# Empty transposes first, token transposes among memory products, rotary tables on GpSimd, and a norm factor kept at -2 times its value

## Chip, core and metric

One core of a Trainium2 chip. The metric is the device time of one launch in microseconds, as the median of several executions. TensorE (PE) does matmuls and transposes, VectorE (DVE), ScalarE (ACT) and GpSimd (POOL) work element by element, and SyncE (SP) issues most of the DMAs.

## What is computed

A decoder trunk of two layers over 1024 tokens of width 1024. Both layers also attend to 256 memory tokens; layer 0 uses latent attention with rotary positions, layer 1 a sliding window. Only the parts that the change touches are quoted.

```python
def rmsnorm(x, g):
    xf = x.astype(jnp.float32)
    y = xf * lax.rsqrt(jnp.mean(xf * xf, axis=-1, keepdims=True) + EPS)
    return (y * g.astype(jnp.float32)).astype(x.dtype)

def rope(x, positions):
    ...
    inv = ROPE_THETA ** (-(jnp.arange(half, dtype=jnp.float32) * 2.0) / r)
    ang = positions.astype(jnp.float32)[..., None] * inv
    cos = jnp.cos(ang)[:, :, None, :]
    sin = jnp.sin(ang)[:, :, None, :]
    ...

def memory_cross_attention(q_cross, mem_n, w_mem_kv):
    b, s, _ = q_cross.shape
    kv = (mem_n @ w_mem_kv).reshape(b, N_MEM, 2, MEM_HEADS, HEAD_DIM)
    ...

    mem_n = rmsnorm(mem, mem_norm_g)
    for i in range(DEPTH):
        j = i // 2
        hn = rmsnorm(x, attn_norm_g[i])
        ...
        cross = memory_cross_attention(q_cross, mem_n, w_mem_kv[i])
        x = x + jnp.concatenate([mix, cross], axis=-1) @ w_o[i]
        x = x + squared_relu_mlp(rmsnorm(x, mlp_norm_g[i]), mlp_w_up[i], mlp_w_down[i])
    return rmsnorm(x, final_norm_g)
```

## The kernel before

Every operand that must be exact is kept as a high and a low half (`split`: ScalarE writes the rounded high half, VectorE the difference), and a product is three matmuls. Tokens stand in eight tiles of 128, weights in slices of 128 rows.

The start. `ident`, the identity for transposes, is built on GpSimd. `mem_T` loads the two memory tiles, transposes a block of 45 rows with all gains (`gains`, from five small DMAs on ScalarE's queue), and for each tile computes the norm factor (`rstd_of`: square with a running sum on ScalarE, mean plus EPS on VectorE, then `newton`), scales it, transposes it in two groups of four and multiplies by the gain on the way out of PSUM. `mem_kv(0)` makes the keys and values of the memory for layer 0: four groups of 16 matmuls in float32, 128x256. Then the first two token tiles are loaded, the input weights `mla_w_in` come slice by slice through two raw buffers and are split, `mem_kv(1)` makes layer 1's memory keys and values, `rope_tables` reduces the angles on VectorE in some 60 small steps and takes two sines on ScalarE, and `masks` builds two masks.

The loop over tokens comes behind that: `a_norm` (factor and scaling), `a_T` (eight transposes, split into `xhls`), `a_in` (the input product, 8 slices of six matmuls into a buffer `ps2` of which there are two; then the norm factors of the compressed parts and the rotation of the key with the tables), `a_cT` (transposes of the result). Buffers `ps1` are four PSUM slots that all small products and transposes share.

Norm factors are a root and a reciprocal with one Newton step, r(1.5 - 0.5 r r z). `Rstd` does the same for the output and MLP phases and for the final norm: `half` squares each half of a row, `get` forms the factor: two sums and EPS on VectorE, root on ScalarE, four small steps on VectorE.

The order on each engine is found at build time by a list scheduler that has its own model of durations; at run time each engine and each DMA queue works strictly in that order. `issue_after` adds an order on one engine, `high_priority` raises a group.

In the kernel's last stage (`Down.run`, layer 1) the final gain is loaded into `gt`; after the last matmul of a token tile come the sum with the residual, the square of the second half, `get`, and a scaling by factor and gain, which is stored.

Of the kernel before, what the change touches and what calls it, by code (L numbers as in the profile page):

```python
# [19 lines left out]
P = 128  # L20
# [35 lines left out]
def trunk(  # L56
# [38 lines left out]

    def split(src, hi, lo, scale=None):

        if scale is None:
            nc.scalar.activation(hi, src, AF.Copy)  # L99
            nc.vector.tensor_tensor(lo, src, f32(hi), ALU.subtract)  # L100
        else:
            nc.scalar.activation(hi, src, AF.Copy, scale=scale)
            nc.vector.scalar_tensor_tensor(lo, src, scale, f32(hi), ALU.mult, ALU.subtract)
# [23 lines left out]

    def masks(pl):

        nc.vector.tensor_copy(identb, ident)  # L130
        for dst, sgn in ((dmask, 1), (dmaskT, -1)):
# [3 lines left out]
            nc.vector.tensor_copy(dst, m)  # L135
# [16 lines left out]
    def gains(pl):  # L152
        grow = pl.tile([45, P], F32, name="grow")
        for src, r in ((mem_norm_g, 37), (attn_norm_g, 0), (mlp_norm_g, 16), (mla_q_norm_g, 32), (mla_kv_norm_g, 35)):
            n = 8 if r == 37 else src.shape[0] * src.shape[1] // P
            nc.scalar.dma_start(out=grow[r : r + n, :], in_=src.rearrange("(k p) -> k p" if len(src.shape) == 1 else "l (k p) -> (l k) p", p=P))
        pt = ps1("psg")[:, 0:45]
        nc.tensor.transpose(pt, grow, ident[0:45, 0:45])
        nc.vector.tensor_copy(gcol, pt)

    small_ct = [0]

    def rstd_of(pl, src_parts, junk):
# [22 lines left out]
    def rstd_halves(pl, xt, junk):  # L186

        small_ct[0] += 1
        ss = pl.tile([P, 2], F32, tag="ss", bufs=4, name=f"ss{small_ct[0]}")
        for i, c in enumerate((slice(0, 512), slice(512, 1024))):  # L190
            nc.scalar.activation(junk[:, c], xt[:, c], AF.Square, accum_out=ss[:, i : i + 1])
        z = pl.tile([P, 2], F32, tag="zs", bufs=4, name=f"zs{small_ct[0]}")[:, 0:1]
        nc.vector.tensor_scalar(z, ss[:, 0:1], ss[:, 1:2], 1.0 / D, ALU.add, ALU.mult)
        nc.vector.tensor_scalar(z, z, EPS, None, ALU.add)
        return newton(pl, ss, z, 1)
# [26 lines left out]
    def rope_tables():  # L222
        tp = pool("ropet")
        V = nc.vector
# [12 lines left out]

        def less(acc, k, c):
            V.scalar_tensor_tensor(acc, k, -c, acc, ALU.mult, ALU.add)

# [9 lines left out]
        def reduced_prod(h, c):  # L250
# [4 lines left out]
            for pc, qc in zip(parts(c, 12, 4), parts(TWO_PI, 12, 4)):  # L255
                V.scalar_tensor_tensor(acc, h, pc, acc, ALU.mult, ALU.add)
# [4 lines left out]
        with tc.issue_after(mem_end[0].ins):  # L261
            V.tensor_copy(posf, pos_i)
# [17 lines left out]
        nc.scalar.activation(sinb.rearrange("p t j -> p (t j)"), th, AF.Sin)  # L280
# [1875 lines left out]
```

## Time and profile before

| | us |
|---|---|
| median of 3 runs | 2117.09 (2114.58 to 2121.81) |
| the profiled execution | 2116.59 |
| its span in the profile | 2114.9 |
| TensorE busy / VectorE / ScalarE / GpSimd | 2078.4 / 1470.6 / 1134.6 / 159.6 |

The page gives for each engine the time in which it worked. TensorE's share says how little can be won, its waits say where, and the windows with the granted clock say where it worked at half speed (0.50 is 1.2 GHz, 1.00 is 2.4 GHz). Matmuls overlap in the records, so the distance between starts, not the duration of one, is their pace.

### The profile page before, as it was taken

Reading aid. Unit: us, or ns where it says so; the run is one execution under the profiler, and the core shown is the slowest. Engines: PE = TensorE matmul, PEld = TensorE weight load, DVE = VectorE, ACT = ScalarE, POOL = GpSimd, SP = SyncE. Lnnn points to the kernel's source line nnn. Section 1 sums busy time; section 2 is a strip of 40 time slices with the busy share of each in tenths; the row PEclk is TensorE's granted clock in tenths of the full one; section 3 lists DMA queues with packets and bytes.
Section 4 is the critical chain, followed back from the end, with each engine's and each line's share of the span. In section 5 each row is a group of like instructions: output and inputs, shape, how many; then the busy total and the mean of one; then the engine's idle time right before and its main releaser. Section 6 shows DMA issues by size and latency. Waiting matters only on the chain.

```text
span 2114.9 us, 29110 instructions
## 1 busy us (share of the span) xinstructions
PE 2078.4 (98%) x9928; PEld 1708.0 (81%) x9928; DVE 1470.6 (70%) x2833; ACT 1134.6 (54%) x2444; POOL 159.6 (8%) x224
## 2 busy tenths in 40 slices
PE   7999999999999999999999999999999999999998
PEld 6988777788788878888888878778888878788886
DVE  7555588865977776976657553866976775976565
ACT  5455477776754443444445553976745443444452
POOL 0013100001000000000001241620000000000000
PEclk9999999999999999999999999999999999999999
DMA  7202123342354446944433241242344446844342
GB/s 247 68 1 76 46 65 92 105 143 100 110 170 162 140 136 218 337 159 143 150 119 95 66 146 54 81 137 73 133 146 159 157 139 230 317 151 155 118 122 85
DMA packets 177070, 282.92 MB, mean 134 GB/s; under 512 B 17581, under 2 KB 73370, under 8 KB 176922
## 3 DMA queue, kind: packets, MB, share of 16 engines
q1 hardware_dynamic: 170480, 265.30, 39.2%
q0 software_dynamic: 4016, 13.12, 1.8%
q10 hardware_dynamic: 2426, 2.65, 0.4%
q8 instruction: 78, 1.28, 0.3%
q14 instruction: 70, 0.57, 0.1%
HBM read 187.47 MB, written 81.05 MB: 127 GB/s over the span
## 4 chain that ended last, share of the span: by engine, by line
PE 80%; DVE 7%; DMA 6%; ACT 4%; issue 2%; SPq 0%; POOL 0%; DVEq 0%; ACTq 0%; POOLq 0%
PE psy L1805 5%; PE psy L1803 5%; PE psy L1804 5%; PE psz L1805 4%; PE psz L1803 4%; PE psz L1804 4%; PE pss L930 4%; PE pso L972 4%; PE psu L1468 3%; PE psu L1470 3%; PE psu L1469 3%; DMA mr<-in_mlp_w_up_dram 3%; PE pswo L108 3%; PE pswo L110 3%; PE pswo L109 2%; PE psf L108 2%
## 5 line engine op out<-in xcount | busy, mean ns | idle before, releaser
L1368 ACT ACTIVATE mr<-mr,gcol 128x256 f32<-128x256 f32 (+1 forms) x160 | 67.3, 477 | 81.2 <-DMA mr<-in_mlp_w_up_dram 77.5
L1368 ACT ACTIVATE d<-d,gcol 128x256 f32<-128x256 f32 x128 | 57.7, 499 | 79.0 <-DMA d<-in_mlp_w_up_dram 61.7
L1803 PE MATMUL psy<-g 128*128 128x512 f32 x256 | 99.9, 390 | 0.0
L1804 PE MATMUL psy<-g 128*128 128x512 f32 x256 | 99.6, 389 | 0.0
L1805 PE MATMUL psy<-g 128*128 128x512 f32 x256 | 99.4, 389 | 0.0
L99 ACT ACTIVATE g<-i 128x512 fp32r<-128x512 f32 x79 | 49.6, 628 | 89.1 <-PE psz L1804 46.3
L100 DVE TENSOR_TENSOR g<-i,g 128x512 fp32r<-128x512 f32 x79 | 55.5, 703 | 48.9 <-ACT g L99 48.9
L99 ACT ACTIVATE uh<-i 128x512 fp32r<-128x512 f32 x66 | 41.6, 630 | 86.1 <-PE psy L1804 40.7
L99 ACT ACTIVATE i<-mr 128x512 fp32r<-128x512 f32 x78 | 49.1, 629 | 70.8 <-PE psy L1804 20.6
L951 ACT ACTIVATE p<-pss 128x512 f32<-128x512 f32 x108 | 63.6, 593 | 41.1 <-PE pss L930 41.0
L100 DVE TENSOR_TENSOR pl<-p,ph 128x512 fp32r<-128x512 f32 (+1 forms) x96 | 61.5, 651 | 27.4 <-ACT ph L99 26.9
L805 DVE TENSOR_REDUCE m<-psx 128x1 f32<-128x128 f32 (+5 forms) x96 | 70.1, 747 | 11.0 <-PE psx L801 10.8
L100 DVE TENSOR_TENSOR uh<-i,uh 128x512 fp32r<-128x512 f32 x66 | 45.6, 690 | 44.7 <-ACT uh L99 44.7
L1804 PE MATMUL psz<-g 128*128 128x512 f32 x192 | 74.7, 389 | 0.0
L1805 PE MATMUL psz<-g 128*128 128x512 f32 x192 | 74.7, 389 | 0.0
L1803 PE MATMUL psz<-g 128*128 128x512 f32 x192 | 74.7, 389 | 0.0
L100 DVE TENSOR_TENSOR i<-mr,i 128x512 fp32r<-128x512 f32 x78 | 53.6, 687 | 22.0 <-ACT i L99 21.6
L1684 DVE TENSOR_TENSOR mqf<-mqq,mqf 128x512 f32<-128x512 f32 x64 | 43.1, 686 | 21.9 <-DMA mqq<-in_mlp_w_down_dram 21.7
L99 ACT ACTIVATE ph<-p 128x512 fp32r<-128x512 f32 (+1 forms) x96 | 56.4, 599 | 1.3
L1805 PEld LDWEIGHTS psy<-g 128*128 128x128 f32 x256 | 48.1, 188 | 10.0
L1804 PEld LDWEIGHTS psy<-g 128*128 128x128 f32 x256 | 48.1, 188 | 9.9
L1803 PEld LDWEIGHTS psy<-g 128*128 128x128 f32 x256 | 48.1, 188 | 9.8
(658 smaller groups left out, 6913.4 us busy)
## 6 DMA issues: line engine op xcount, KB each, us to landing
i<-hd SPq DMA_DIRECT2D x154, 256.0 KB
hd<-uh SPq DMA_DIRECT2D x76, 256.0 KB
hd<-ul SPq DMA_DIRECT2D x76, 256.0 KB
mr<-in_mlp_w_up_dram SPq DMA_DIRECT2D x36, 512.0 KB
hd<-x SPq DMA_DIRECT2D x72, 256.0 KB
mr<-hd SPq DMA_DIRECT2D x70, 256.0 KB
d<-in_mlp_w_up_dram SPq DMA_DIRECT2D x32, 512.0 KB
mqq<-in_mlp_w_down_dram SPq DMA_DIRECT2D x32, 512.0 KB
```

What stands on the lines that cost most here:

```text
L99: nc.scalar.activation(hi, src, AF.Copy)
L100: nc.vector.tensor_tensor(lo, src, f32(hi), ALU.subtract)
L108: nc.tensor.matmul(ps, ah, bh, start=first and i == 0, stop=False)
L110: nc.tensor.matmul(ps, al, bh, start=False, stop=last and i == n - 1)
L805: nc.vector.reduce_max(m8s[h][:, i : i + 1], ps[:, c], axis=AX, negate=True)
L930: return lambda: nc.tensor.matmul(o, a, b, skip_group_check=True, **kw)
L951: nc.scalar.activation(p, ps, AF.Exp, scale=SC)
L972: mms.append(lambda: nc.tensor.matmul(o, a, b, skip_group_check=True, **kw))
L1368: nc.scalar.activation(w[:, k, :], w[:, k, :], AF.Copy, scale=g_mlp[layer][:, k0 + k : k0 + k + 1])
L1803: nc.tensor.matmul(ps, ah[:, j, :], bh, start=p in (1, 5, 2) and k == 0, stop=False, skip_group_check=True)
L1804: nc.tensor.matmul(ps, ah[:, j, :], bl, start=False, stop=False, skip_group_check=True)
L1805: nc.tensor.matmul(ps, al[:, j, :], bh, start=False, stop=k == NP - 1, skip_group_check=True)
```

## The change

Transposes: `idle(n)` transposes the identity n times into a PSUM buffer that nobody reads: 24 ahead of everything, 10 between the two memory tiles, 8 ahead of the memory products. The memory's gains are loaded and transposed on their own first. The first two token tiles are normalised ahead of the weight splits and transposed between the groups of `mem_kv(1)`, whose weight loads are issued behind the fourth input slice; raw buffers for input weights become four; tokens 2 and 3 are loaded right behind the weights. The masks are built at the start and cast behind the memory tiles.

Rotary tables: all steps go to GpSimd, a fused multiply-add becomes two steps, and the two sines are put behind the last memory copy, the last split and the last root on ScalarE.

Norm factors: the root is taken from the sum itself (scale and EPS inside the activation), the Newton step becomes (t - 3) r, which is -2 times the factor, and all gains are scaled by -0.5. `Rstd` adds EPS to the first half's sum on GpSimd, feeds that to the root of the second sum as its bias, and forms z on GpSimd.

```diff
+    ends = [None, None]
+
     def split(src, hi, lo, scale=None):
 
         if scale is None:
-            nc.scalar.activation(hi, src, AF.Copy)
+            ends[1] = nc.scalar.activation(hi, src, AF.Copy)
...
+    built = []
+
     def masks(pl):
 
-        nc.vector.tensor_copy(identb, ident)
         for dst, sgn in ((dmask, 1), (dmaskT, -1)):
             m = pl.tile([P, P], F32, tag="mask", bufs=2, name=f"mask{sgn}")
             nc.gpsimd.memset(m, 0.0)
             nc.gpsimd.affine_select(out=m, in_=m, compare_op=ALU.is_ge, fill=NEG, base=0, pattern=[[-sgn, P]], channel_multiplier=sgn)
-            nc.vector.tensor_copy(dst, m)
+            built.append((dst, m))
+
+    def masks_cast():
+        with tc.issue_after(mem_end[0].ins):
+            nc.vector.tensor_copy(identb, ident)
+            for dst, m in built:
+                nc.vector.tensor_copy(dst, m)
...
+    def gains(pl, srcs, at, name):
+        n = sum(int(np.prod(src.shape)) // P for src in srcs)
+        grow = pl.tile([n, P], F32, name=f"grow{name}")
+        r = 0
+        for src in srcs:
+            k = int(np.prod(src.shape)) // P
+            nc.scalar.dma_start(out=grow[r : r + k, :], in_=src.rearrange("(k p) -> k p" if len(src.shape) == 1 else "l (k p) -> (l k) p", p=P))
+            r += k
+
+        def turn():
+            pt = ps1(f"psg{name}")[:, 0:n]
+            nc.tensor.transpose(pt, grow, ident[0:n, 0:n])
+            nc.vector.tensor_scalar(gcol[:, at : at + n], pt, -0.5, None, ALU.mult)
+
+        return turn
...
+    root = [None]
 
     def rstd_of(pl, src_parts, junk):
 
         k = len(src_parts)
         small_ct[0] += 1
-        ss = pl.tile([P, 2], F32, tag="ss", bufs=4, name=f"ss{small_ct[0]}")
-        z = pl.tile([P, 2], F32, tag="zs", bufs=4, name=f"zs{small_ct[0]}")
+        ss, z, rs, t = [pl.tile([P, 2], F32, tag=n, bufs=4, name=f"{n}{small_ct[0]}") for n in ("ss", "zs", "rs", "rt")]
         for i, (ap, n) in enumerate(src_parts):
-            nc.scalar.activation(junk[:, :n], ap, AF.Square, accum_out=ss[:, i : i + 1])
-            nc.vector.tensor_scalar(z[:, i : i + 1], ss[:, i : i + 1], 1.0 / n, EPS, ALU.mult, ALU.add)
-        return newton(pl, ss, z[:, :k], k)
-
-    def newton(pl, ss, z, k):
-
-        rs = pl.tile([P, 2], F32, tag="rs", bufs=4, name=f"rs{small_ct[0]}")
-        rk, t = rs[:, :k], ss[:, :k]
-        nc.scalar.activation(t, z, AF.Sqrt)
+            c = slice(i, i + 1)
+            nc.scalar.activation(junk[:, :n], ap, AF.Square, accum_out=ss[:, c])
+            root[0] = nc.scalar.activation(t[:, c], ss[:, c], AF.Sqrt, scale=1.0 / n, bias=eps_t)
+            nc.vector.tensor_scalar(z[:, c], ss[:, c], 1.0 / n, EPS, ALU.mult, ALU.add)
+        rk, t, z = rs[:, :k], t[:, :k], z[:, :k]
         nc.vector.reciprocal(rk, t)
-        nc.vector.tensor_tensor(t, rk, rk, ALU.mult)
-        nc.vector.tensor_tensor(t, t, z, ALU.mult)
-        nc.vector.tensor_scalar(t, t, -0.5, 1.5, ALU.mult, ALU.add)
-        nc.vector.tensor_tensor(rk, rk, t, ALU.mult)
+        if k == 1:
+            nc.vector.scalar_tensor_tensor(t, rk, z, rk, ALU.mult, ALU.mult)
+        else:
+            nc.vector.tensor_tensor(t, rk, rk, ALU.mult)
+            nc.vector.tensor_tensor(t, t, z, ALU.mult)
+        nc.vector.scalar_tensor_tensor(rk, t, -3.0, rk, ALU.add, ALU.mult)
         return rs
...
-        V = nc.vector
+        V = nc.gpsimd
...
+        def add(acc, k, c):
+            n[0] += 1
+            r = tp.tile([P, NT * 16], F32, tag="add", bufs=2, name=f"rt{n[0]}")
+            V.tensor_scalar(r, k, c, None, ALU.mult)
+            V.tensor_tensor(acc, acc, r, ALU.add)
+
         def less(acc, k, c):
-            V.scalar_tensor_tensor(acc, k, -c, acc, ALU.mult, ALU.add)
+            add(acc, k, -c)
...
+        with tc.issue_after(ends[0].ins), tc.issue_after(ends[1].ins), tc.issue_after(root[0].ins):
+            nc.scalar.activation(sinb.rearrange("p t j -> p (t j)"), th, AF.Sin)
+            nc.scalar.activation(hs, th, AF.Sin, scale=0.5)
...
+    def mem_kv_steps(layer, kv, memT, pl):
...
+            ends[0] = nc.scalar.activation(kv.v[:, t, :], ps, AF.Copy)
+            yield
...
-        gains(pl)
+        turns = [gains(pl, [mem_norm_g], 37, "m"), gains(pl, [attn_norm_g, mlp_norm_g, mla_q_norm_g, mla_kv_norm_g], 0, "")]
+        turns[0]()
         for t in range(2):
             y = pl.tile([P, D], F32, tag="y", bufs=2, name=f"ym{t}")
-            rs = rstd_of(pl, [(xs[t], D)], y)
+            with tc.issue_after(root[0].ins):
+                rs = rstd_of(pl, [(xs[t], D)], y)
             nc.vector.tensor_scalar(y, xs[t], rs[:, 0:1], None, ALU.mult)
+            if t:
+                idle(10)
             for a in range(0, KT, 4):
                 ps = ps1(f"psTm{t}_{a}")
                 for i in range(4):
                     nc.tensor.transpose(ps[:, i * P : (i + 1) * P], y[:, (a + i) * P : (a + i + 1) * P], ident)
                 mem_end[0] = nc.vector.tensor_tensor(mT[:, a : a + 4, t * P : (t + 1) * P], ps.rearrange("p (k c) -> p k c", k=4), g_mem[:, a : a + 4].unsqueeze(2).to_broadcast([P, 4, P]), ALU.mult)
+        turns[1]()
+        idle(8)
         return mT
...
+    root[0] = nc.scalar.activation(warm, eps_t, AF.Sqrt)
+    def idle(n):
+        pw = ps1(f"psnone{n}")
+        for _ in range(n):
+            nc.tensor.transpose(pw[:, 0:P], ident, ident)
+
+    idle(24)
+    masks(pm)
     memT = mem_T(pm)
     small_loads()
     mem_kv(0, kv0, memT, pm)
...
+    def a_norm(t):
+        norm_y(pa, xts[t], fa0[:, 2 + t % 2, :])
+        if 1 < t < NT - 2:
+            xts.append(load_x(t + 2))
...
     xts = [load_x(0), load_x(1)]
+    a_norm(0)
+    a_norm(1)
     wih = pa.tile([P, KT, MLA_IN], F32R, name="wih")
     wil = pa.tile([P, KT, MLA_IN], F32R, name="wil")
     for kt in range(KT):
-        raw = f1[:, kt % 2, 0:MLA_IN]
+        raw = f1[:, kt % 4, 0:MLA_IN]
         nc.sync.dma_start(out=raw, in_=mla_w_in[0, kt * P : (kt + 1) * P, :])
         split(raw, wih[:, kt, :], wil[:, kt, :], scale=g_attn[0][:, kt : kt + 1])
-    mem_kv(1, kvt, memT, pm)
+        if kt == 3:
+            mem1 = mem_kv_steps(1, kvt, memT, pm)
+            next(mem1)
+    xts += [load_x(2), load_x(3)]
+    for t, _ in enumerate(mem1):
+        if t < 2:
+            a_T(t)
+    a_norm(2)
+    masks_cast()
     rope_tables()
-    masks(pm)
...
-    a_norm(0)
-    for k in range(NT + 2):
-        if k < NT:
+    for k in range(1, NT + 2):
+        if 1 < k < NT:
             a_T(k)
-        if k + 1 < NT:
+        if 1 < k < NT - 1:
             with tc.high_priority(offset=120):
                 a_norm(k + 1)
...
+            self.n = 0
+
+        def half(self, x_, junk):
+            ss = self.st[:, self.n : self.n + 1]
+            nc.scalar.activation(junk, x_, AF.Square, scale=1.0 / 32.0, accum_out=ss)
+            if self.n == 0:
+                nc.gpsimd.tensor_scalar(self.st[:, 5:6], ss, EPS, None, ALU.add)
+            self.n += 1
 
         def get(self):
-            ss, z, rk, t = self.st[:, 0:2], self.st[:, 2:3], self.st[:, 3:4], self.st[:, 4:5]
-            nc.vector.tensor_scalar(z, ss[:, 0:1], ss[:, 1:2], EPS, ALU.add, ALU.add)
-            nc.scalar.activation(t, z, AF.Sqrt)
+            ss, z, rk, t, z0 = [self.st[:, i : i + 1] for i in (1, 2, 3, 4, 5)]
+            nc.scalar.activation(t, ss, AF.Sqrt, bias=z0)
+            nc.gpsimd.tensor_tensor(z, ss, z0, ALU.add)
             nc.vector.reciprocal(rk, t)
             nc.vector.scalar_tensor_tensor(t, rk, z, rk, ALU.mult, ALU.mult)
-            nc.vector.tensor_scalar(t, t, -0.5, 1.5, ALU.mult, ALU.add)
-            nc.vector.tensor_tensor(rk, rk, t, ALU.mult)
+            nc.vector.scalar_tensor_tensor(rk, t, -3.0, rk, ALU.add, ALU.mult)
             return rk
...
             if layer == 1:
                 gt = m.raw()
                 nc.scalar.dma_start(out=gt.rearrange("p a c -> p (a c)"), in_=final_norm_g.partition_broadcast(P))
+                nc.gpsimd.tensor_scalar(gt, gt, -0.5, None, ALU.mult)
```

In `rope_tables` the other fused multiply-add (acc + h pc) is `add(acc, h, pc)` too, and `posf` no longer waits for the memory tiles. The definitions of `xhls`, `a_norm` and `a_T` move up unchanged but for the line shown; `rstd_halves`, which nothing called, goes.

## Rows read from the trace of the kernel before

**Rows 1.** The page, part 1: busy us, share of the span, instructions.
```profile
PE 2078.4 (98%) x9928; PEld 1708.0 (81%) x9928; DVE 1470.6 (70%) x2833; ACT 1134.6 (54%) x2444; POOL 159.6 (8%) x224
```

**Rows 2.** Waits of TensorE over the span: total us, times, longest us.
```profile
PE psg L158 <- DMA grow<-in_mla_kv_norm_g_dram: 9.7, 1, 9.7
PE psT_a L207 <- DVE kml L334: 2.4, 2, 1.6
...
PE psT_m L1286 <- ACT d L1275: 1.2, 2, 1.0
```

**Rows 3.** TensorE in order of time, 0 to 64: start us, us, count.
```profile
9.90 3.55 PE L444 MATMUL psTm<-ident,ym 128*128 128x128 f32 x16
13.50 7.17 PE L319 MATMUL pskm<-memT,wm 128*128 128x256 f32 x32
...
34.33 7.07 PE L326 MATMUL psvm<-wm,memT 128*128 128x256 f32 x32
...
47.64 0.78 PE L117 MATMUL psin<-wih,xhls 128*128 128x512 f32 x1
...
56.68 0.39 PE L117 MATMUL psin<-wih,xhls 128*128 128x512 f32 x1
...
57.94 0.39 PE L117 MATMUL psin<-wih,xhls 128*128 128x512 f32 x1
```

**Rows 4.** The chain that ended last, in order of time: start us, us.
```profile
59.36 0.87 PE psT_a L207 x8
```

**Rows 5.** Windows: us, busy by engine, granted TensorE clock, DMA share, GB/s.
```profile
48.00:50.00 2.00, 2.00 (x6) 1.68 (x6) 0.84 (x3) 1.97 (x4) 0.00 (x0) 0.50 0.83 260
```

**Rows 6.** GpSimd, ScalarE and VectorE in order of time, 0 to 62.
```profile
2.24 0.31 POOL L125 TENSOR_SCALAR_AFFINE_SELECT ident<-ident 128x128 f32<-128x128 f32 x1
...
4.55 1.06 ACT L170 ACTIVATE ym<-mem 128x1024 f32<-128x1024 f32 x1 [1.62 <-DMA mem<-in_mem_dram]
...
7.08 0.52 ACT L178 ACTIVATE ss<-zs 128x1 f32<-128x1 f32 x2
...
8.39 0.86 DVE L440 TENSOR_SCALAR ym<-mem,rs 128x1024 f32<-128x1024 f32 x1
...
12.76 1.42 DVE L445 TENSOR_TENSOR memT<-psTm,gcol 128x512 f32<-128x512 f32 x2 [0.16 <-PE psTm L444]
...
15.10 0.17 DVE L262 CAST posf<-pos_i 128x8 f32<-128x8 int32 x1 [0.93 <-DMA pos_i<-in_positions_dram]
...
30.59 1.18 DVE L103 SCALAR_TENSOR_TENSOR wil<-fa,gcol,wih 128x928 fp32r<-128x928 f32 x1 [1.69 <-ACT wih L102]
```

**Rows 7.** Windows of 20 us, the first: columns as in rows 5.
```profile
0.00:20.00 20.00, 10.29 (x47) 9.21 (x48) 11.23 (x59) 8.09 (x15) 2.60 (x15) 1.00 0.95 286
```

**Rows 8.** GpSimd's groups by shape: count, busy us, mean ns, idle before.
```profile
L303 POOL TENSOR_TENSOR fa<-fa,rb 128x192 f32<-128x192 f32 x8 | 5.7, 711 | 0.0
...
L1976 POOL CAST df<-di 128x128 f32<-128x128 int32 x1 | 0.3, 287 | 0.0
```

**Rows 9.** Instructions on the rotary tables: ns min/median/max, first and last start.
```profile
L239 DVE SCALAR_TENSOR_TENSOR rt<-rt,rt x18: 272/285/293, 17.1 to 40.1; 128x128 f32<-128x128 f32 x18
...
L256 DVE SCALAR_TENSOR_TENSOR rt<-rt,rt x8: 283/285/288, 17.9 to 33.0; 128x128 f32<-128x128 f32 x8
```

**Rows 10.** Instructions that read the cosine table, the first group of rotations.
```profile
L298 DVE TENSOR_TENSOR fa<-psin,cosb x8: 168/174/175, 68.2 to 145.6; 128x16 f32<-128x16 f32 x8
```

**Rows 11.** All engines in order of time, around 1120.
```profile
1120.19 0.48 DVE L1785 TENSOR_SCALAR d<-g,sinb 128x512 f32<-128x512 f32 x1
...
1120.53 1.89 POOL L1902 TENSOR_TENSOR wsr<-wsr,gcol 128x1024 f32<-128x1024 f32 x1 [3.18 <-DMA wsr<-in_swa_w_in_dram]
1120.58 2.12 DVE L1785 TENSOR_SCALAR d<-d,sinb 128x512 f32<-128x512 f32 x1
```

**Rows 12.** VectorE in order of time, the last norm factor.
```profile
2108.58 0.21 DVE L1199 TENSOR_SCALAR cosb<-cosb 128x1 f32<-128x1 f32 x1 [0.79 <-ACT i L1195]
...
2109.52 0.15 DVE L1203 TENSOR_SCALAR cosb<-cosb 128x1 f32<-128x1 f32 x1
```

More of the change, by code (lines that the diff above doesn't have):

```diff
@@ L150, in trunk @@
     g_q, g_kv, g_mem = gcol[:, 32:35], gcol[:, 35:37], gcol[:, 37:45]
[L152 to L159, printed above, removed]
+    def gains(pl, srcs, at, name):
[11 more added lines that the diff above has]
+        return turn
     small_ct = [0]
+    root = [None]
     def rstd_of(pl, src_parts, junk):
@@ L255, in reduced_prod @@
             for pc, qc in zip(parts(c, 12, 4), parts(TWO_PI, 12, 4)):
-                V.scalar_tensor_tensor(acc, h, pc, acc, ALU.mult, ALU.add)
+                add(acc, h, pc)
                 less(acc, k, qc)
@@ L260, in rope_tables @@
         posf = tp.tile([P, NT], F32, name="posf")
-        with tc.issue_after(mem_end[0].ins):
-            V.tensor_copy(posf, pos_i)
+        V.tensor_copy(posf, pos_i)
         ang = tmp()
@@ L309, in mem_kv @@
     def mem_kv(layer, kv, memT, pl):
+        for _ in mem_kv_steps(layer, kv, memT, pl):
+            pass
+    def mem_kv_steps(layer, kv, memT, pl):
         wsrc = w_mem_kv[layer].rearrange("(k p) n -> p k n", p=P)
@@ L322, in mem_kv @@
                 dup_split(ps[e * 64 : e * 64 + 64], kv.kh[:, h, :], kv.kl[:, h, :])
+        yield
         for t in range(2):
@@ L326, in mem_kv @@
                 nc.tensor.matmul(ps, memT[:, kt, t * P : (t + 1) * P], wv[:, kt, :], start=kt == 0, stop=kt == KT - 1)
-            nc.scalar.activation(kv.v[:, t, :], ps, AF.Copy)
+            ends[0] = nc.scalar.activation(kv.v[:, t, :], ps, AF.Copy)
+            yield
     def dup_split(ps, kh, kl):
@@ L473, in trunk @@
     warm = pm.tile([P, 1], F32, name="warm")
-    nc.scalar.activation(warm, eps_t, AF.Sqrt)
+    root[0] = nc.scalar.activation(warm, eps_t, AF.Sqrt)
[5 more added lines that the diff above has]
+    masks(pm)
     memT = mem_T(pm)
@@ L485, in load_x, with a_T @@
         return xt
+    xhls = quad_tile("q0", "xhls", F32R)
+    xT, cs_ = {}, {}
+    def a_norm(t):
+        norm_y(pa, xts[t], fa0[:, 2 + t % 2, :])
+        if 1 < t < NT - 2:
+            xts.append(load_x(t + 2))
+    def a_T(t):
+        y = fa0[:, 2 + t % 2, :]
+        xhl = [xhls[:, 2 * (t % 2) + i, :].rearrange("p (k c) -> p k c", k=KT) for i in range(2)]
+        xh, xl = xhl
+        T_split(y, lambda a: (xh[:, a : a + 4], xl[:, a : a + 4]), f"a{t}")
+        xT[t] = (xh, xl)
     xts = [load_x(0), load_x(1)]
+    a_norm(0)
+    a_norm(1)
     wih = pa.tile([P, KT, MLA_IN], F32R, name="wih")
@@ L537, in trunk @@
     CQC, CKR = 640, 896
-    xhls = quad_tile("q0", "xhls", F32R)
-    xT, cs_ = {}, {}
-    def a_norm(t):
-        norm_y(pa, xts[t], fa0[:, 2 + t % 2, :])
-        if t + 2 < NT:
-            xts.append(load_x(t + 2))
-    def a_T(t):
-        y = fa0[:, 2 + t % 2, :]
-        xhl = [xhls[:, 2 * (t % 2) + i, :].rearrange("p (k c) -> p k c", k=KT) for i in range(2)]
-        xh, xl = xhl
-        T_split(y, lambda a: (xh[:, a : a + 4], xl[:, a : a + 4]), f"a{t}")
-        xT[t] = (xh, xl)
     def a_in(t):
@@ L1192, in __init__ @@
             self.st = st[:, small_ct[0] % 8, :]
-        def half(self, i, x_, junk):
-            nc.scalar.activation(junk, x_, AF.Square, scale=1.0 / 32.0, accum_out=self.st[:, i : i + 1])
+            self.n = 0
[5 more added lines that the diff above has]
+            self.n += 1
         def get(self):
-            ss, z, rk, t = self.st[:, 0:2], self.st[:, 2:3], self.st[:, 3:4], self.st[:, 4:5]
-            nc.vector.tensor_scalar(z, ss[:, 0:1], ss[:, 1:2], EPS, ALU.add, ALU.add)
-            nc.scalar.activation(t, z, AF.Sqrt)
+            ss, z, rk, t, z0 = [self.st[:, i : i + 1] for i in (1, 2, 3, 4, 5)]
+            nc.scalar.activation(t, ss, AF.Sqrt, bias=z0)
+            nc.gpsimd.tensor_tensor(z, ss, z0, ALU.add)
             nc.vector.reciprocal(rk, t)
             nc.vector.scalar_tensor_tensor(t, rk, z, rk, ALU.mult, ALU.mult)
-            nc.vector.tensor_scalar(t, t, -0.5, 1.5, ALU.mult, ALU.add)
-            nc.vector.tensor_tensor(rk, rk, t, ALU.mult)
+            nc.vector.scalar_tensor_tensor(rk, t, -3.0, rk, ALU.add, ALU.mult)
             return rk
@@ L1272, in norm @@
             t = TORD[p]
-            rst[t].half(1, xb, y[:, 1, :])
+            rst[t].half(xb, y[:, 1, :])
             rs = rst.pop(t).get()
@@ L1317, in sum0 @@
                 rst[t] = Rstd()
-                rst[t].half(0, x_, m.t(f"d{3 + p % 2}")[:, 0, :])
+                rst[t].half(x_, m.t(f"d{3 + p % 2}")[:, 0, :])
             xs = {0: load(0, half), 1: load(1, half)}
@@ L1733, in stat @@
                     nc.gpsimd.dma_start(out=x1[ts, i * 512 : i * 512 + 512], in_=xs[i])
-                    r.half(i, xs[i], y[i])
+                    r.half(xs[i], y[i])
                 def fin():
@@ L1780, in norm @@
                 for i in (1, 0):
-                    r.half(i, xs[i], y[i])
+                    r.half(xs[i], y[i])
                 rs = r.get()
```

11 lines of the change are left out of this document (removed).

## The prediction

> **What bounds the kernel now.** I read the page first: TensorE is busy for 98% of the span [rows 1], so only time in which it stands still, or runs at the lower clock, can be won. Next the waits of TensorE over the whole span, longest first [rows 2]: one of 9.7 us before its first instruction, 2.4 us ahead of the first token transposes, and from there on nothing above 1.2 us in one place. The change touches the start, the norm factors all along and the end, so I then read the start in order of time, with the clock. Three things are to be seen there. First, the 16 memory transposes take 3.55 us [rows 3], 0.222 us each, where eight token transposes later take 0.87 us [rows 4], 0.109 each: they run at 1.2 GHz, though the clock column shows no drop so early. The memory products follow without a gap from 13.50 to 41.40 [rows 3]. Second, between 41.40 and the third token's transposes at 59.36 [rows 3, 4] lie 17.96 us, in which TensorE does 16 transposes and one token's input product. At full speed that is 16 x 0.109 = 1.74, and eight steps of 57.94 - 56.68 = 1.26 us, 10.08: together 11.82. So 6.1 us are lost: part as waits for PSUM buffers that a crowded VectorE frees late [rows 2], the rest because the granted clock after them is 0.50 (1.2 GHz), as late as 50 [rows 5]. Third, the memory tokens: ScalarE starts the first square at 4.55, but both roots come at 7.08, behind the second square, and the first normalised tile is written only at 8.39 [rows 6].
>
> **The change, part by part.** The sum is made against the profiled execution, 2116.59 us, span 2114.9, so 1.69 lie around the span; it is 0.5 below the median of the three runs, 2117.09.
>
> *Start of the memory products, 13.50 now.* The square of tile 0 ends at 4.55 + 1.06 = 5.6, some 5.7 with its sum. The root now follows it, with no VectorE step between: 0.25, then three small steps of about 0.2 each [rows 12], then 0.86 for the tile [rows 6]: 7.4 to 7.5 instead of 9.25. Its eight transposes take 0.9 at the full clock. Tile 1's root is where both were, 7.08 plus its time; its factor is there at 8.0 and the tile at 8.8, its transposes done at 9.7. From 7.5 on VectorE has tile 1's small steps (0.6), its scaling (0.86) and four multiplications by the gain, 0.71 each (1.42 for two, [rows 6]); the first product needs three of these four: 11.1, the last is done at 11.8. I take 11.3. Bounds: 10.0 if only tile 1's first multiplication follows its transposes, 12.3 if all 42 empty transposes stand ahead of the 16 real ones (2.55 + 24 x 0.222 + 18 x 0.109 + 1.74 + 0.71). The 24 first ones start when the identity is ready, at 2.55 [rows 6]; at 0.222 they end by 7.9, and sooner once the clock rises. TensorE has nothing else to do then, so I cost them at nothing; without that cover the 42 cost 42 x 0.109 = 4.6. The gain row for the memory now has its own transpose, ahead of tile 0: if that small DMA lands as late as the last of the five did (9.7, [rows 2]), 2 us of this part are gone. Gain 2.2, between 0.2 (that) and 3.5.
>
> *From there to the third token's transposes.* Memory products 27.9, 16 token transposes 1.74, one input product 10.08: 39.7 with no wait, so 11.3 + 39.7 = 51.0 instead of 59.36. The token transposes now stand between products, which hide the emptying of their PSUM buffers: the 6.1 us lost there should not come back. Gain of both parts together 8.4.
>
> *Is the data there?* SyncE's queue now has, ahead of the second layer's memory keys: 1.05 MB memory, 2.1 MB first memory weights, 1.05 MB tokens, 1.9 MB input weights; with the keys 7.15 MB. At the 286 GB/s of the first 20 us [rows 7] they have landed at 25.0; their halves are needed at 25.2 and 26.1. The rest, to the last input weight (10.1 MB), lands at 35.3 and is split by 37.6; the input product needs its first step at 40.9 and its last after 49. So it fits, with about 1 us to spare in the first place.
>
> *Rotary tables on GpSimd.* VectorE is rid of 26 multiply-adds of 0.285 [rows 9] and the other steps on the tables. [...] Up to the sine: 16 small columns and 41 steps with one input, at no more than 0.29, and 28 with two. For these the trace has 0.29 (one input, same size) and 0.71 (two inputs, half as wide again) as ends [rows 8]; I take 0.45, nearer by size. 57 x 0.29 + 28 x 0.45 = 29.1 us from the landing of the positions, 15.10 [rows 6]: 44.2, by the ends 39.7 to 51.5. Sine, its table and two closing steps add 2.6. The first rotation stands at 68.2 now [rows 10], at 59.8 after a shift of 8.4, and the third input product needs its PSUM buffer back at about 62.7. So the tables are hidden, by 6 to 17 us. Behind the sines on ScalarE's queue stand the squares and roots of token 0 and the high halves of token 2: they have the same slack. Roots and sines still alternate once, so table loads are as many as now.
>
> Against this part speaks what happens when GpSimd and VectorE read together: a 128x512 scaling takes 0.48 us at 1120.19 and 2.12 at 1120.58, where a GpSimd product of 1.89 began 0.05 earlier [rows 11]. So whichever starts second may wait for the whole of the other. In the window VectorE has eight low halves of the input weights, 1.18 each, and three scalings of 0.86 [rows 6]: at most 12 us that GpSimd can lose, so the angles come at 56.2 at worst from 44.2, and at 63.5 from 51.5; only the last would show, with 6 us. The Trainium skill, "SBUF — State Buffer", section "Who interferes with whom", says this as a rule: the port pair that VectorE and GpSimd share is an exclusive lock, taken for the whole instruction by VectorE instructions with two SBUF inputs or in a two-port mode; by that rule, with which the trace agrees at 1120.58, GpSimd loses time to every such instruction, and rival C is how far that could go.
>
> *Norm factors.* At the end of the kernel the chain from the last sum to the scaled tile loses one VectorE step of 0.21 with its hop (0.25) and one of 0.15 (0.18) [rows 12]; one product becomes a fused step, +0.06. Gain 0.37, nothing hides it. GpSimd's addition runs beside root and reciprocal. The other factors lie beside matmuls; what they can shorten is TensorE's wait for a normalised tile, 1.2 us in two places [rows 2]. I take 0, bounds 0 and +1.2. The added GpSimd steps stand behind GpSimd's queue: at the end of layer 0 it waits up to 3.18 us for weights and then works 1.89 [rows 11], and a factor queued behind that is late by up to 5. There is no wait of TensorE in the waits view there now and several matmul steps of cover, so 0, bound -3. The factor -2 is taken out in gains that are scaled anyway; the last gain costs one GpSimd step beside matmuls.
>
> Sum: 8.4 + 0.4 = 8.8; 2116.59 - 8.8 = **2107.8**.
>
> **The rivals.**
> *The wait moves (B).* ScalarE and VectorE take their work in order; a weight split placed ahead of a PSUM copy waits for its DMA and holds the copy back, or the keys come 1 to 2 us after 25.2. Then TensorE stops among the second layer's products and the clock falls as it does now. For: the spare of 1 us, and that today's waits [rows 2] are of this kind. Against: four raw buffers and an emptier VectorE. Half of today's 6.1 plus 1.3 us of waiting: gain 4.4, **2112.2**.
>
> *Tables too late (C), the slower side.* ScalarE's sine waits for GpSimd; all that follows it on that queue waits too. It decides from a sine at 60; every microsecond later is one of TensorE, and at 69 the gain is gone. If each of the 69 full-size steps loses 0.6 us to VectorE (half a weight split), the angles come at 85.6, the closing steps at 88: 28 lost, **2136**. Against: it needs 41 us of lock where I count 12.
>
> *The empties don't raise the clock, or wait in each other's way (D).* Then the memory products start at 1.2 GHz, as the 16 transposes do now: about 1.8 us less, **2109.6**.
>
> *Waits of the middle go as well (E).* 1.2 for the normalised tiles and 1 at the start: **2105.6**.
>
> **How the numbers follow.** Forecast 0.62, B 0.20, C 0.06, D 0.05, E 0.07. A measurement of this kernel tells about 0.3% from no change, 6.4 us: below 2110.7 is faster. Forecast, D and E are: 0.74; B lies within: 0.20; C is slower: 0.06. The range takes in forecast, D, E and most of B with the bounds of the start: 2105.0 to 2113.0.
>
> **What would show it.** Memory transposes at 0.109 each and the first memory product near 11.3; no idle time of TensorE and no 0.50 in the clock column between 41 and 51; the third token's transposes near 51.0; the last sine before 55 on ScalarE and the first rotation near 60; the closing chain 0.37 shorter. Wrong would be: a first product after 12.7, a wait of TensorE for memory keys, or ScalarE idle for GpSimd while TensorE idles for ScalarE.

## The result and the profile after

The changed kernel takes 2126.62 us (median of 6 runs, 2123.93 to 2127.94), the kernel before 2118.32 in the same set of runs: ratio 1.0039, 95% interval 1.0028 to 1.0051. It is slower by 8.3 us, where the forecast was 8.8 faster. The profiled execution has a span of 2125.0, 10.1 longer than before.

The page, part 1 (columns as in [rows 1]), then the waits of TensorE with the largest totals (as in [rows 2]):

```profile
PE 2087.1 (98%) x9971; PEld 1713.5 (81%) x9971; DVE 1449.3 (68%) x2678; ACT 1141.6 (54%) x2452; POOL 229.6 (11%) x379
```

```profile
PE pskm L334 <- DVE memT L466: 5.6, 1, 5.6
...
PE psu L1510 <- ACT d L1549: 3.8, 7, 1.1
PE psct L611 <- DVE fa L599: 2.8, 1, 2.8
```

VectorE lost 21 us of work and GpSimd took on 70, as meant. The two longest waits of [rows 2] are gone, and two new ones of several us each stand there (`pskm` and `psct`; the row between them is seven waits of at most 1.1 in the two up projections). The first is at the head of the memory products. TensorE in order of time, to be held against [rows 3]:

```profile
1.69 5.38 PE L501 MATMUL psnone<-ident 128*128 128x128 f32 x24 [1.69 <-POOL ident L127]
...
7.35 1.10 PE L465 MATMUL psTm<-ident,ym 128*128 128x128 f32 x8
...
9.70 1.45 PE L465 MATMUL psTm<-ident,ym 128*128 128x128 f32 x8 [0.16 <-DVE gcol L173]
...
17.98 10.20 PE L334 MATMUL pskm<-memT,wm 128*128 128x256 f32 x32 [5.61 <-DVE memT L466]
28.02 7.07 PE L342 MATMUL psvm<-wm,memT 128*128 128x256 f32 x32
...
60.54 1.03 PE L211 MATMUL psT_a<-ident,fa 128*128 128x128 f32 x8
```

Both memory tiles are turned by 11.2, before by 13.5 [rows 3], and once the last empty transposes are through nothing runs for 5.6 us. The products that follow take 10.20 in place of 7.07: after the idle time the clock is at its lower level, which costs another 3.1. VectorE shows why, with the ScalarE line that it waits for (second fence):

```profile
9.75 1.29 DVE L466 TENSOR_TENSOR memT<-psTm,gcol 128x512 f32<-128x512 f32 x2
16.39 0.15 DVE L190 TENSOR_SCALAR zs<-ss 128x1 f32<-128x1 f32 x1 [5.35 <-ACT fa L188]
...
17.24 1.28 DVE L466 TENSOR_TENSOR memT<-psTm,gcol 128x512 f32<-128x512 f32 x2
```

```profile
15.20 1.06 ACT L188 ACTIVATE fa<-fa 128x1024 f32<-128x1024 f32 x1 [7.06 <-DMA fa<-in_x_dram]
```

The norm factor of token 0 stands in VectorE's queue between the second and the third of the four multiplications by the gain, two for each memory tile. It needs a token that lands at 15.2; the two multiplications behind it had their input at 11 and wait with it.

The second new wait follows from the tables. ScalarE in order of time, and TensorE where it waits:

```profile
51.10 1.28 ACT L291 ACT_TABLE_LOAD   x1
60.02 0.31 ACT L291 ACTIVATE sinb<-rt 128x128 f32<-128x128 f32 x1 [7.64 <-POOL rt L288]
...
64.84 0.51 ACT L104 ACTIVATE wkvh<-wr,gcol 128x256 fp32r<-128x256 f32 x1 [2.71 <-DMA wr<-in_mla_w_ukv_dram]
...
65.66 0.47 ACT L188 ACTIVATE fa<-psin 128x384 f32<-128x384 f32 x1
```

```profile
74.39 1.04 PE L611 MATMUL psct<-ident,fa 128*128 128x128 f32 x7 [2.75 <-DVE fa L599]
```

```profile
76.00:78.00 2.00, 2.00 (x10) 2.00 (x9) 0.88 (x4) 2.00 (x8) 0.00 (x0) 0.50 0.57 152
```

The last fence is a window (columns as in [rows 5]). ScalarE stands at the sine for 7.64 us, with six weight splits and the squares behind it. A raw weight's buffer is free for the next transfer only when it is split, so the transfers start late too (2.71 at 64.84), and the square of token 0's input product, whose matmuls end at 60.7, starts at 65.66. TensorE then waits 2.75 for the normalised parts, and the clock drops to 0.50.

Where the 10.1 us come from, as the lag of the trace of after behind that of before at the same instruction: layer 1's memory keys +7.5, third token's transposes +1.35 (59.19 before; the chain of [rows 4] puts them at 59.36), end of the input products +6.3, first up product of layer 0 +5.2, last one +10.8, last one of layer 1 +11.0, end of the last matmul +10.5, end +10.1. So there are two losses, 6.3 in the first 146 us, and 5.6 in the up projection of layer 0, where the forecast had nothing; 1.5, 1.3 and 0.4 are won, at the output projections of the two layers and at the end, and most of the 1.3 is lost again by the last up product of layer 1.

### The profile page after: what moved, and what is told of

It is laid out like the page before. It is cut to its first block, busy times and chain, and to the rows that moved or that the text cites. A ratio compares the mean times of both kernels' runs of the same rounds, so it can differ in the third digit from the quotient of the medians.

```text
span 2125.0 us, 29262 instructions
## 1 busy us (share of the span) xinstructions
PE 2087.1 (98%) x9971; PEld 1713.5 (81%) x9971; DVE 1449.3 (68%) x2678; ACT 1141.6 (54%) x2452; POOL 229.6 (11%) x379
## 4 chain that ended last, share of the span: by engine, by line
PE 73%; DMA 9%; DVE 7%; ACT 5%; POOL 2%; issue 2%; SPq 0%; DVEq 0%; ACTq 0%; POOLq 0%
PE psy L1846 5%; PE psy L1848 5%; PE psy L1847 5%; PE psz L1846 4%; PE psz L1848 4%; PE psz L1847 4%; DMA mr<-in_mlp_w_up_dram 4%; PE pss L968 4%; PE pso L1010 3%; DMA d<-in_mlp_w_up_dram 3%; PE pswo L112 3%; PE pswo L110 3%; PE pswo L111 3%; PE psu L1510 2%; PE psu L1512 2%
## 5 line engine op out<-in xcount | busy, mean ns | idle before, releaser
L843 DVE TENSOR_REDUCE m<-psx 128x1 f32<-128x128 f32 (+5 forms) x96 | 70.2, 748 | 11.0 <-PE psx L839 10.8
L1945 POOL TENSOR_TENSOR wsr<-wsr,gcol 128x1024 f32<-128x1024 f32 x12 | 23.9, 1990 | 358.8 <-DMA wsr<-in_swa_w_in_dram 358.8
L1395 POOL DMA_DIRECT2D xd<-i x32 | 18.6, 582 | 355.1 <-DVE i L1357 272.1
L1848 PEld LDWEIGHTS psy<-g 128*128 128x128 f32 x256 | 48.1, 188 | 10.1
```

Of the source, the lines that this page charges most:

```text
L843: nc.vector.reduce_max(m8s[h][:, i : i + 1], ps[:, c], axis=AX, negate=True)
L1848: nc.tensor.matmul(ps, al[:, j, :], bh, start=False, stop=k == NP - 1, skip_group_check=True)
```

## The experiments

All times are medians, each ratio is against the kernel before on the same chip (its medians there: 2117.96 for e1 to e4, 2118.66 for e5 to e8, 2117.93 for e9 and e10, 2117.74 for the rest).

| run | edit, in words | us | ratio, 95% interval |
|---|---|---|---|
| e1 | after, token norms behind the memory tiles | 2126.79 | 1.0036 (1.0024 to 1.0049) |
| e2 | after, tables on VectorE | 2119.64 | 1.0007 (0.9998 to 1.0016) |
| e3 | e1 and e2 | 2120.27 | 1.0009 (1.0000 to 1.0018) |
| e4 | before, with the new root alone | 2118.65 | 1.0002 (0.9994 to 1.0011) |
| e5 | e1, sines later on ScalarE | 2123.08 | 1.0021 (1.0013 to 1.0030) |
| e6 | after, with the old root | 2127.76 | 1.0046 (1.0033 to 1.0059) |
| e7 | e5, GpSimd's steps in the two-operation form | 2117.09 | 0.9995 (0.9987 to 1.0004) |
| e8 | before, again | 2118.90 | 1.0007 (0.9999 to 1.0016) |
| e9 | e7, tables in other memory | 2115.95 | 0.9987 (0.9978 to 0.9995) |
| e10 | e9, memory values in the wide buffers | 2109.70 | 0.9962 (0.9948 to 0.9975) |
| e11 | e9, token norms ahead again | 2118.03 | 1.0004 (0.9995 to 1.0013) |
| e12 | e10, with the old root | 2113.59 | 0.9984 (0.9975 to 0.9993) |

**e1, the order on VectorE.**

```diff
-    a_norm(0)
-    a_norm(1)
+    with tc.issue_after(mem_end[0].ins):
+        a_norm(0)
+        a_norm(1)
```

> The changed kernel with one edit: the norms of tokens 0 and 1 are queued on VectorE behind the last memory gain multiplication. Theory: the late start came from VectorE's fixed order, in which token 0's norm factor (waiting 5.35 us for a square whose tile landed at 15.2) stood ahead of two of the four memory tiles; so the first memory product should go from 17.98 to about 12, its 32 products from 10.20 to about 7.1 us, some 8 us in all. The tables on GpSimd don't get earlier by it, so ScalarE should wait longer for the sine and give part of it back: about 2121, between 2118 and 2123. Rival: the products wait for their weights or the clock falls anyway; then the first product stays behind 16 and the time at 2126 to 2127.

The start did as the theory says, the time did not move. TensorE, then its longest wait in the first 140 us, a window behind it, and ScalarE:

```profile
11.64 7.07 PE L334 MATMUL pskm<-memT,wm 128*128 128x256 f32 x32
...
37.66 3.69 PE L342 MATMUL psvm<-wm,memT 128*128 128x256 f32 x16 [2.75 <-issue]
```

```profile
PE psct L612 <- DVE fa L600: 8.4, 1, 8.4
```

```profile
72.00:76.00 4.00, 0.91 (x5) 0.94 (x6) 3.94 (x17) 1.29 (x5) 0.00 (x0) 0.50 0.44 118
```

```profile
60.70 0.31 ACT L291 ACTIVATE sinb<-rt 128x128 f32<-128x128 f32 x1 [13.29 <-POOL rt L288]
```

The first input product starts at 45.3, 2.3 ahead of before and 5.0 ahead of after. But the angles come at 60.7 whatever TensorE does. ScalarE now waits 13.29 for them, TensorE 8.4 in place of 2.75, and the clock is at 0.50 for longer: the input products end 7.3 behind before. So the late start was real, and cost nothing as long as the tables set the end. I had expected some 2.5 us to be given back; it was all of it, as far as the times tell (the interval of either ratio is some 0.0025 wide, 5 us).

**e2 and e3, tables back on VectorE.** The function's engine is VectorE again, with fused multiply-adds; in e3 with e1's edit.

```diff
-        V = nc.gpsimd
+        V = nc.vector
-            V.tensor_scalar(r, k, c, None, ALU.mult)
-            V.tensor_tensor(acc, acc, r, ALU.add)
+            V.scalar_tensor_tensor(acc, k, c, acc, ALU.mult, ALU.add)
```

> The changed kernel with the rotary tables back on VectorE in fused multiply-adds; token norms left where the change has them. Theory: the sine at 60.0 held ScalarE's queue for 7.6 us and cost about 5 us behind it (third stage, 74.4: wait 2.75 and half clock); with the angles ready earlier these go, while the late start stays: about 2121.5, between 2120 and 2123. Rival: the wait at 74.4 comes from the weight split that waits for its transfer (wr), or the 60 table steps on VectorE delay the splits of tokens 0 and 1 as much; then 2125 to 2129.

> The changed kernel with both edits. Theory: both losses of the start go, 8 and 5 us: about 2113.5, between 2111 and 2116, that is 4 to 5 us faster than the kernel before, with the first input product near 45 and no table wait on ScalarE. Rival: on VectorE tables and norms crowd each other once nothing waits; then 2117 to 2122. What the middle of the kernel loses (about 5 us in the up projection of layer 0) should stay in either case.

e2 gains 7.0, more than expected: nearly the whole loss hung on the tables. e3 is not faster than e2; the rival holds. Its first product is at 11.40, but VectorE, with tables, weights and keys to do, empties the keys' PSUM buffers late, and TensorE waits 6.07 ahead of layer 1's memory values. That this is a wait for those buffers was not tested in e3; in e10, where the values use other buffers and stand earlier, the like wait is gone:

```profile
40.53 5.62 PE L340 MATMUL psvm<-wm,memT 128*128 128x256 f32 x16 [6.07 <-issue]
```

**e4, e6 and e8, the middle.** e4 is the kernel before with the third part alone, e6 the changed kernel without it, e8 the kernel before once more. In e4 layer 1's attention gain isn't scaled by -0.5, so values differ from there on; no instruction is less.

```diff
-            nc.vector.tensor_scalar(z, ss[:, 0:1], ss[:, 1:2], EPS, ALU.add, ALU.add)
-            nc.scalar.activation(t, z, AF.Sqrt)
+            nc.scalar.activation(t, ss, AF.Sqrt, bias=z0)
+            nc.gpsimd.tensor_tensor(z, ss, z0, ALU.add)
```

> The kernel before with only the third part of the change: the output stages' norm factor with the root from the second sum, the partial sum and the factor's z on GpSimd, and the factor of -2 undone in gains scaled by -0.5. Theory: this part reorders the queues of the MLP behind it and so causes the 5.5 us lost in layer 0's up projection; it gains 1.3 in each of the two output projections and 0.4 at the end: about 2118.3 + 2.5 = 2121, between 2119 and 2123. Rival: the up projection loses by the later start or by another part, and this part alone gains: about 2118.3 - 3.0 = 2115.3, between 2114 and 2117.

> The changed kernel with the root of the kernel before in the output stages (both sums first, six steps on VectorE), the factor of -2 kept by 1.0 and -3.0 in place of -0.5 and 1.5. Theory: the root alone changed nothing that can be measured (e4, ratio 1.0002), so this stays at 2126 to 2128.5: the start carries the whole loss. Rival: in the changed kernel the new root costs the 4 to 5 us of the up projection; then this comes down to 2122 to 2124.

> The kernel before, unchanged, profiled and timed as the others are. It measures how far one profiled execution differs from the next in the up projection of layer 0, where the kernels with the new root ran 3.1 to 5.6 us longer than the one profile of before. Theory: most of that is how the transfers of the weights happen to fall in one execution, since the queues of ScalarE and SyncE are the same there in the kernel before and in e4 from the second step on: its up projection ends 1 to 4 us later than in the first profile, and the ratio is 1.000 within 0.001. Rival: the loss is the new root's; then this profile repeats the first within 0.5 us.

e4's time is that of before, between theory and rival. e6 stays as slow as after, so the root is not what made it slow. How long the up projection of layer 0 takes, from its first to its last product: 310.0 in the first profile of before, 311.5 in e8, 313.1 in e4, 315.6 in after, 314.6 in e6, 312.8 to 314.2 in the others. The 1.5 of e8 is no measure of the rest, against its theory: there the clock fell at the start of the stage (first fence, a window of e8), which costs 1.3 in the first 32 products, and from then on e8 keeps within 0.7 of that. In the changed kernels the clock is at 1.00 all through the stage, and they lose 2.8 to 5.6 us in it, with either root. Of the 5.6 in after some 3 are waits of TensorE ahead of these products, 5.1 us in all against 2.2 before (second fence: two rows of after that grew; third: the first of the two in before; both within the stage). I can't name their cause: the order on SyncE's queue is the same in all of them, and the order on ScalarE's differs from before's, but for one place, in the first 60 us of the stage only.

```profile
540.00:550.00 10.00, 8.56 (x38) 6.94 (x39) 8.49 (x19) 9.10 (x20) 0.54 (x1) 0.83 0.08 31
```

```profile
PE psu L1510 <- ACT i L1549: 1.3, 5, 0.4
PE psu L1510 <- DVE x L1562: 1.1, 1, 1.1
```

```profile
PE psu L1468 <- ACT i L1507: 0.2, 1, 0.2
```

**e5 and e7, the sine's place and GpSimd's form.** In e5 the sines are called in the first `a_in`, behind its roots; e7 adds a second operation to the one-operation steps.

```diff
-        with tc.issue_after(ends[0].ins), tc.issue_after(ends[1].ins), tc.issue_after(root[0].ins):
-            nc.scalar.activation(sinb.rearrange("p t j -> p (t j)"), th, AF.Sin)
+        def sines():
+            with tc.issue_after(root[0].ins):
+                nc.scalar.activation(sinb.rearrange("p t j -> p (t j)"), hs, AF.Sin)
```

```diff
-            V.tensor_scalar(r, k, c, None, ALU.mult)
+            V.tensor_scalar(r, k, c, 0.0, ALU.mult, ALU.add)
```

> The kernel of experiment e1 (token norms behind the memory tiles, which started its products at 11.64 but gained nothing in all) with one more edit: the two sines are queued on ScalarE behind the roots of token 0's normalised parts instead of ahead of the weight splits; the tables stay on GpSimd, as late as before. Theory: in e1 ScalarE stood at the sine from 47.4 to 60.7 (13.29 us) and this alone turned a start 2.3 us earlier into an end of the third stage 7.3 us later; so 9 us come back: about 2118, between 2115 and 2120, and no wait at the first transposes of token 0's parts. Rival: what is held up is the rotation itself, which needs the angles at 60 wherever the sine is queued; then the wait at the parts' transposes stays over 2 us and the time above 2122.

> The kernel of e5 with GpSimd's one-operation multiplications of the table chain written with a second operation that adds zero (32 of them, 128x128). Theory: the two-operation form took 0.30 us in the changed kernel's trace and the one-operation form 0.53 to 0.55; the chain gets about 32 x 0.24 = 7.7 us shorter and the angles stand near 52 instead of 60: about 2116.5, between 2114 and 2119. Rival: the long times come from what VectorE does beside it, not from the form; then the steps stay near 0.53, the angles at 60, and the time is that of e5.

e5's time is the rival's, and TensorE still waits 2.55 for token 0's parts; but its reason is neither. ScalarE of e5, then of e7:

```profile
60.67 0.51 ACT L104 ACTIVATE wknh<-wr,gcol 128x256 fp32r<-128x256 f32 x1 [9.18 <-POOL cosb L289]
```

```profile
55.07 0.51 ACT L104 ACTIVATE wknh<-wr,gcol 128x256 fp32r<-128x256 f32 x1 [5.73 <-POOL cosb L289]
```

With the sine out of the way, a weight split waits for the last table step. It reads nothing of the tables; the split weights take over memory that the tables' pool gives back, which e9 tests. GpSimd's table steps (line, count, ns min/median/max) in after, then in e7, where L239 adds twice and L245 multiplies and adds:

```profile
L238 POOL TENSOR_SCALAR rt<-rt x6: 299/300/1032, 15.8 to 53.8; 128x128 f32<-128x128 f32 x6
...
L239 POOL TENSOR_SCALAR rt<-rt x6: 529/540/552, 16.1 to 54.2; 128x128 f32<-128x128 f32 x6
...
L245 POOL TENSOR_SCALAR rt<-rt x26: 529/531/1762, 16.8 to 57.6; 128x128 f32<-128x128 f32 x26
...
L246 POOL TENSOR_TENSOR rt<-rt,rt x26: 447/457/1275, 17.8 to 58.8; 128x128 f32<-128x128 f32 x26
```

```profile
L239 POOL TENSOR_SCALAR rt<-rt x6: 657/1066/1589, 16.1 to 50.1; 128x128 f32<-128x128 f32 x6
...
L245 POOL TENSOR_SCALAR rt<-rt x26: 294/298/1086, 16.9 to 52.9; 128x128 f32<-128x128 f32 x26
```

The theory on the form holds for multiply-and-add, 0.53 to 0.30, and not for two additions: 0.54 becomes 0.66 where nothing large of VectorE's runs beside the step (two of the six), and more in the other four. The chain ends 5.6 sooner, not 7.7, and the time falls by 6.0.

**e9, e10, the two waits that were left.** e9 puts the tables' tiles into the memory of the first layer's queries. e10 lets layer 1's memory values use the two wide PSUM buffers, ahead of token 1's transposes.

```diff
-        tp = pool("ropet")
+        tabs = quad_tile("q1", "ropeq").rearrange("p a (b c) -> p (a b) c", c=NT * 16)
```

```diff
-            ps = ps1(f"psvm{layer}_{t}")[:, :256]
+            ps = (ps2 if layer else ps1)(f"psvm{layer}_{t}")[:, :256]
```

> The kernel of e7 with the tables' intermediate tiles in the memory of the first layer's queries (written from 68 us on) in place of a pool of their own, whose memory the split weights wkn take over once it is released. Theory: the wait that moved from the sine to the weight split in e5 and e7 (9.18 and 5.73 us, ended by GpSimd's last table step) is this reuse of memory, not the sine and not the rotation; it goes, the third stage keeps its start 2.8 us ahead to its end, and the half-clock stretch at 150 to 170 (1.3 us) may go with it: about 2114.5, between 2112.5 and 2116.5, the first version faster than the kernel before. Rival: the splits wait for the weights' transfers instead and the first transposes of the parts wait as before; then it stays with e7 at 2116.5 to 2118.

> The kernel of e9 with layer 1's memory values accumulated in the two wide PSUM buffers that the input products use later, both ahead of token 1's transposes. Theory: the 2.6 us that TensorE idled ahead of the first of them (37.1 in e7) are a wait for one of four narrow buffers, held until VectorE has read the keys; the values then follow token 0's transposes at once and the first input product starts near 42.5 instead of 44.8: about 2112.3, between 2110.5 and 2114.5. Rival: token 0's split or the last weight split on VectorE is not done by then and the input product starts where it did; then the time is that of e9.

Both moved as the theories said, e10 by more. In e9 the second split follows the first at 51.18, TensorE has no wait for the parts any more, the clock stays at 1.00 from 60 to 180, and e9 is a little faster than before. So the wait of e5 and e7 was for the memory. What that is worth is not shown: the intervals of e7 and e9 overlap, and e9's traced execution is 1.3 longer than e7's. In e10 layer 1's values run without a gap, and the first input product is at 42.07, 5.6 ahead of before [rows 3]. TensorE of e10:

```profile
11.58 7.07 PE L337 MATMUL pskm<-memT,wm 128*128 128x256 f32 x32
...
34.37 7.07 PE L345 MATMUL psvm<-wm,memT 128*128 128x256 f32 x32
...
42.07 0.47 PE L119 MATMUL psin<-wih,xhls 128*128 128x512 f32 x1
...
52.22 1.03 PE L211 MATMUL psT_a<-ident,fa 128*128 128x128 f32 x8
```

e10 is the fastest version: 2109.7, 0.38% under the kernel before and 16.9 us under the changed one.

**e11 and e12, parts taken back from versions without the table wait.** e11 is e9 with the token norms ahead again, e12 is e10 with the old root, by the edits shown for e1 and e4, turned round.

> The kernel of e9 with the first edit taken back: token 0's and 1's norms stand on VectorE where the change put them, ahead of two memory tiles. Theory: the late start (5.6 us idle, then half clock) showed no price in e1 only because ScalarE's wait behind it set the end; with that wait gone it costs what e9 gained at the head: the first product at 18 again, the first input product 4 to 6 us later than e9's 46.7, the whole 2120 to 2122. Rival: the start is made good elsewhere (token 1's transposes and layer 1's values wait anyway) and the time stays within 1.5 of e9's 2116.

> The kernel of e10, the fastest so far, with the root of the kernel before in the output stages (as in e6). Theory: the new root gains what the milestones show, 1.3 at each of the two output projections and 0.4 at the end: so 3 us slower than e10, about 2112.7, between 2111 and 2114.5. Rival: its reordering of the up projections takes the gain back; then it is within 1 us of e10's 2109.7 or faster.

e11 has the late start again (first product 17.32 after 5.42 us of idle time), and costs 2.1 (3.6 by the two ratios, from two sets of runs): less than the theory's 4 to 6. Its first input product comes only 2.9 later than e9's, since e9's own wait among layer 1's products (2.69 at 37.42) is not there when they come late. e12 costs 3.9, between its theory's 3 and the end of its range. In the traces of e10 and e12 the stretch from the last output product to the first up product of layer 0 is 1.9 against 3.3, and the one to layer 1's last transposes 6.7 against 8.0: 2.7 from the root itself. The two traces are 5.6 apart, but 3.6 of that is there before the first output product (443.6 against 440.0), ahead of the root's first use: the clock fell twice on the way in e12, and not in e10 (last section). So the traces leave 2.0 to 2.7 to the root; how much of the medians' 3.9 is clock, no run shows.

## Why the prediction was wrong, point by point

- **Start of the memory products: the step failed.** The squares, roots and transposes came as worked out (the first tile's transposes start at 7.35, forecast 7.4 to 7.5), and the empties did raise the clock (eight memory transposes take 1.10, sixteen took 3.55 before): rival D is out. I followed the memory tiles' own chain on VectorE and never asked what else of the change is queued there. Token 0's norm, moved ahead, stands among them and waits for a token; its landing at 15.2 was to be read from my own sum of transfers (3.15 MB are ahead of the tokens; at the 286 GB/s of [rows 7] that is 11.0 before the first byte of theirs). Without it (e1) the first product is at 11.64, forecast 11.3.
- **From there to the third token: right.** 17.98 plus the 39.7 of the forecast plus 3.1 of half clock is 60.8; the trace has 60.54. The 6.1 us lost before between 41 and 59 are gone. Rival B appeared once the start was right: 2.75 at 37.66 in e1, a wait for PSUM buffers. With that removed too, e10 has the third token at 52.22, forecast 51.0.
- **Tables on GpSimd: the step that decided.** The angles came at 60.0, forecast 44.2, bound 51.5 before the time lost to VectorE and 63.5 with it. The full-size steps began 4.0 ahead of the forecast (15.76 for 15.10 + 16 x 0.29), and from there 69 steps took 44.2 us; the forecast for them was 41 x 0.29 + 28 x 0.45 = 24.5. Of the 19.7 too many, 32 one-operation steps at 0.53 instead of 0.29 make 7.7, about 4.3 are the pauses between steps that each wait for the last (some 0.06 each, which I left out), and about 7 are time lost to VectorE: 17.4 - 26 x 0.53 = 3.6 on L245, and as worked out in the same way 1.5 on L246, 1.0 on L238 and 0.8 on the scaling of the sinks queued among them. I had bounded the last by 12. My 0.29 was the row of a type cast of that size [rows 8]; the trace had no one-operation step of that size to show, and I took the nearest row for an upper end.
- **The slack of the sine: mis-sized.** Rival C was the right mechanism, with chance 0.06 and the wrong point of decision. I had it decide from a sine at 60, at one for one, and the sine came at 60.02; the cost was already 5. I read the slack from who needs the angles. The queue has more in it: ahead of the squares stand weight splits that need no angle, their transfers wait for the buffers, and a memory pool waits for the last table step (e5). e2 prices all of it at 7.0 us.
- **Norm factors.** The end of the kernel is 0.4 shorter, forecast 0.37. In the middle I took 0 with +1.2 as the bound; the root gains 1.5 and 1.3 at the two output projections, of which the second does not last. That GpSimd's queue might hold a factor back (bound -3) did not show.
- **The up projection of layer 0: not in the forecast.** I put this stage at nothing, without a reason. It took 5.6 us more in the trace of after, at full clock, and 2.8 or more in every changed kernel. Some 3 of the 5.6 are waits ahead of its products; what makes them longer stays open.

What VectorE's reads do to a table step is in one line of GpSimd: the step began while VectorE was at a weight split that reads two tiles (20.01 to 21.18, with a scaling behind it to 21.89), and took 1.76 instead of 0.53.

```profile
20.26 1.76 POOL L245 TENSOR_SCALAR rt<-rt 128x128 f32<-128x128 f32 x1
```

The Trainium skill, "SBUF — State Buffer", section "Who interferes with whom", has it that a VectorE instruction with two SBUF inputs contends with a GpSimd instruction that reads SBUF, over a port pair that is an exclusive lock. The trace agrees: the step, begun 0.25 into the split, ended only at 22.02, behind split and scaling.

## What to carry to other kernels

Engines work their queues in order: when a step is moved ahead, read when its input lands and which ready work stands behind it, on every queue that it touches. A chain moved to another engine is late for its readers, for everything queued behind the instruction that waits for it, and for whoever gets its memory next; price it by rows of the very form and size, with the pauses between dependent steps. A part judged alone can look worthless while another wait sets the end (e1: nothing; taken back in e11: 2.1; the root in e4: nothing, in e12: 3.9, by the traces at least 2.0), so take the parts back once more from the best version.

## What the runs showed of the hardware

- On GpSimd a 128x128 scalar step with one operation takes 0.53 us, with a multiplication and an addition 0.30 (medians of after and e7), with two additions 0.66 where it runs undisturbed (e7).
- The same short wait may or may not lower the clock. Of the kernel before there are two traces: behind waits of 1.0 and 0.9 us at 540 and 542 the granted clock stayed at 1.00 in the first, and fell in e8. Behind 1.06 us of idle time at 153, with the same work around it, it was 1.00 in e10 and fell in e12 (first two windows, columns as in [rows 5]); e12 is 1.6 us further behind after that stretch. In e12 it fell once more behind 1.93 us at 419 (third window), where e10 waits 1.43 and keeps its clock.

```profile
150.00:160.00 10.00, 8.45 (x63) 7.03 (x62) 5.92 (x12) 8.11 (x33) 6.73 (x4) 1.00 0.01 2
```

```profile
150.00:160.00 10.00, 8.45 (x54) 6.79 (x54) 5.59 (x11) 7.63 (x32) 5.68 (x3) 0.83 0.01 2
```

```profile
420.00:425.00 5.00, 5.00 (x24) 4.14 (x24) 1.73 (x6) 2.56 (x5) 0.00 (x0) 0.69 0.24 75
```
